# The order of a quad's seven products, and of their weights

## The chip, the cores and the metric

The kernel runs on one core of one Trainium2 chip. Its time is the device time of one execution in microseconds (us), given as the median of several runs; lower is better. A profile is one further execution, recorded by the hardware profiler.

Engines are named as in the profile: PE is the matrix engine and PEld its loading of weights, DVE the vector engine, ACT the scalar engine, POOL the general engine, SP the engine that issues most transfers. Matrix products build up in eight banks of PSUM, each 128 partitions by 512 floats.

## The reference

One layer of a streaming encoder over 2048 tokens of 1024 features, all in float32. An input projection feeds a chunked band attention and an mLSTM, both gated; their sum goes through an output projection, and a feed-forward block of width 4096 follows.

```python
xn = rms_norm(x, mix_norm_g)
proj = xn @ w_in
aq, ak, av, mq, mk, mv, mo, ipre, fpre, ga, gm = jnp.split(proj, points, axis=-1)
att = chunk_band_attention(aq, ak, av, rel_bias)
...
mlstm_out = sigmoid(mo) * rms_norm(mlstm_chunkwise(conv(mq), conv(mk), mv, ipre, fpre))
y = sigmoid(ga) * (att @ w_att_proj) + sigmoid(gm) * (mlstm_out @ w_mlstm_proj)
x = x + y @ w_out
hn = rms_norm(x, ffn_norm_g)
x = x + jnp.square(jax.nn.relu(hn @ w_up)) @ w_down
```

## The kernel before, in words

The tokens are cut into four blocks of 512. Blocks 0 and 1 form one span, blocks 2 and 3 the other. The large products of a span (gates, the second span's input projections, output projection, up and down projection) are computed by Winograd's form of Strassen's scheme: a product of 2 x 2 blocks by seven products in place of eight. Each float32 operand is split in two parts, high and low, and each product takes three matmuls.

**A quad** (`quad`, L731, matmul at L753) is one such set of seven products: 0 to 6. For one product it takes one weight tile (`next_w`), runs over two halves n of the output features, over four tiles k of the inner dimension and over the three pairs of parts: 24 matmuls of 128 x 512. A product goes to banks named by `PLACES` (L64): product 0 to x, 1 to y, 2 to z, 3 to x, 4 to z, 5 and 6 to x. A place has two banks, one for each half. Products that share a place add to what stands there; before such a product begins, what the place held must have been taken out (the event `clear`). Order of the seven products before: 0, 1, 2, 3, 4, 5, 6, so places x y z x z x x.

**Emptying the banks** (`combine`, L1876). After products 0, 2 and 3 ACT copies the bank to a buffer of the pool `ctx` (L1887). After products 1, 4 and 5 DVE adds the bank to one of these copies (L1895): 1 to the copy of 0, 4 to the copy of 3, 5 to the copy of 2. Product 6 is the last output. Banks y are given back after product 1, z after 4, x after 6. For the output projection (`after_out`, L2074) DVE adds the bank to a tile of x in place of the copy (L2109).

**A token quad** (`quad_tok`, L760, matmul at L781) computes values of the attention and the mLSTM. It differs in that a product needs two weight tiles, and goes through both halves first with one tile and then with the other.

**Weights.** A weight tile of a product is 128 x 1024. ACT casts it to its high part (L608) and DVE subtracts to get the low part (L610, `split_now`); the result lies in one of three buffers `wsp`. Its source lies in one of four buffers `wraw`. Where a quad's weights come from raw tiles (`quad_w`, L614), four tiles a, b, c, d are loaded (L567) and the sums that the scheme needs are made in place by four DVE subtractions (L627), between the splits. In six quads of the first up projection (`kept`) each sum is also written to HBM (L622), and the tile is overwritten only after that. Other quads load ready tiles one by one (`part`); their sums were made earlier by `sum_w` (L544, subtractions at L559), which DVE does in between. `weights` (L479) lists all tiles in the order in which PE takes them.

**Order of the work.** Threads (generators) run in a simulated flow with estimated costs (`Flow`). That gives buffers and the order on PE. Then `Order` (L212) lists each other engine's instructions anew, by due times counted back from PE and with margins, and fixes that order; each engine works through its list in order, SP's transfers too.

**Stages with quads:** four gate quads of span 0 (`ga0`, `ga1`, `gm0`, `gm1`), two output quads, eleven of span 1's input (`gm0`, `gm1`, `q`, `mq`, the token quad `vm0`, `ga0`, `k`, the token quad `vm1`, `mk`, `ga1`, `mo`), eight up quads, then after the down projection two output quads and eight up quads of span 1. In all 33 quads and two token quads, 168 matmuls each. In a stage's first quad the operands come in while it runs. The down projection (matmuls at L669 to L671) is worked otherwise.

Of the kernel before, what the change touches and what calls it, by code (L numbers as in the profile page):

```python
# [57 lines left out]
EARLY_SUMS.update({i: N_Q - N_F + n for n, i in enumerate((7, 9, 11, 12, 13, 14, 15, 16))})  # L58

ORDER = (0, 1, 3, 2, 5, 4, 6)  # L60
N_RING = 8
LAST = (3, 1)

# [309 lines left out]
class Layer:  # L373
# [105 lines left out]
    def weights(self):  # L479


        part = lambda q, m: ("part", (q, m))
        quad = lambda name: ("quad", (int(name[2]) if name[:2] == "gm" else Q_IN[name], False))
        proj = [("plain", N_W - 8 + 4 * x + j) for j in (0, 2, 1, 3) for x in range(2)]
        rows = lambda *k: [("plain", 8 + 5 * j + i) for j in range(4) for i in k]
        mv = [("plain", n) for n in range(4, 8)]
        for b in range(2):
            yield from (("plain", n) for n in range(4))
            yield from mv + rows(0, 1) if b == 0 else rows(0, 1) + mv
            yield from rows(2, 3) + rows(4)  # L490
        yield from proj
        for name in GATES:
            yield quad(name)
        yield from proj
        yield from (part(q, m) for q in range(N_G, N_G + N_O) for m in range(7))
        for name in IN_ORDER:
            if name[:2] == "vm":
                yield from (part(Q_VM + kk, m) for m in range(7) for kk in range(2))
            else:
                yield quad(name)  # L500
        for s in range(NS):
            if s == 1:
                yield from (part(q, m) for q in range(N_G, N_G + N_O) for m in range(7))
            for q in range(N_G + N_O, N_G + N_O + N_F):
                if s == 0 and q >= N_G + N_O + N_USUM:
                    yield "quad", (q, True)
                else:
                    yield from (part(q, m) for m in range(7))
            for p, m in enumerate(ORDER):
                for q in range(N_Q - N_F, N_Q):  # L510
                    yield part(q, m)
            if s == 0:
                yield from proj + proj

    def loader(self):
        fl, io = self.fl, self.io
        i = 0
        for kind, n in self.weights():
            if kind == "quad":
                raws, evs = [], [Event() for _ in range(4)]  # L520
                fl.spawn(self.quad_w(i, *n, raws, evs), 0)
                for j in range(4):
                    (raw,) = yield "get", self.wraw, 1
                    raws.append(raw)
                    fl.spawn(self.load_w(io["wf"][n[0], j], raw, evs[j]), 0)
                i += 7
                continue
            first = kind == "plain" and i < KT // 2
            if kind == "plain":
                src = io["w"][n]  # L530
            else:
                q, m = n
# [78 lines left out]
        self.wtile[i] = w  # L611
        fl.set(self.wev[i])

    def quad_w(self, i, q, kept, raws, evs):  # L614


        fl, V = self.fl, self.nc.vector
        spilt = [Event() for _ in range(4)]

        def keep(n, raw):  # L620
            yield "sp", 1750, 2000
            self.nc.sync.dma_start(self.td[q].ap()[n], raw)  # L622
            fl.set(spilt[n])

        def sub(n, dst, x, y):
            yield "dve", dve_ns(1024)
            V.tensor_sub(dst, x, y)  # L627
            if kept:
                fl.spawn(keep(n, dst), 1)
            else:  # L630
                fl.set(spilt[n])

        yield "wait", [evs[0]]
        a = raws[0]
        yield from self.split_now(i, a)
        yield "wait", [evs[1]]
        b = raws[1]
        yield from sub(0, a, b, a)
        yield "wait", [evs[2]]
        c = raws[2]  # L640
        yield from self.split_now(i + 1, c)
        yield from self.split_now(i + 2, a)
        yield "wait", [evs[3], spilt[0]]
        d = raws[3]
        yield from sub(1, a, d, a)
        yield from self.split_now(i + 3, a)
        yield from self.split_now(i + 4, d)
        yield from sub(2, b, d, b)
        fl.put(self.wraw, d, late=self.LATE)
        yield "wait", [spilt[1]]  # L650
        yield from sub(3, a, c, a)
# [76 lines left out]
        fl.put(self.wsplit, w, late=self.LATE_SPLIT)  # L728
        return got

    def quad(self, A, aev, after, release):  # L731


        fl = self.fl
        bank, clear = {}, {}
        mm = self.nc.tensor.matmul
        for m, z in enumerate(PLACES):
            w = yield from self.next_w()
            wv = w.rearrange("p a (k n c) -> p a k n c", k=4, n=2)
            for n in range(2):  # L740
                new = (z, n) not in bank
                if new:
                    (bank[z, n],) = yield "get", self.banks, 1
                else:
                    yield "wait", [clear[z, n]]
                ps = bank[z, n]
                for k in range(4):
                    if aev[m][k] is not None:
                        yield "wait", [aev[m][k]]
                    yield "pe", 681  # L750
                    a = A[m][k]
                    for x, y in ((0, 0), (0, 1), (1, 0)):
                        mm(ps, wv[:, x, k, n], a[:, y], start=new and k == 0 and x == y == 0,  # L753
                           stop=k == 3 and x == 1, skip_group_check=True)
                clear[z, n] = after(m, n, ps)
            fl.put(self.wsplit, w, late=self.LATE_SPLIT)
            if release:
                fl.put(self.rpool, *A[m])

    def quad_tok(self, p, A, aev, after):  # L760
# [1 line left out]
        fl = self.fl  # L762
        bank, clear = {}, {}
        mm = self.nc.tensor.matmul
        for m, z in enumerate(PLACES):
            for kk in range(2):
                w = yield from self.next_w()
                wv = w.rearrange("p a (k c) -> p a k c", k=2)
# [44 lines left out]
    def dense(self):  # L813
# [59 lines left out]
        for i, name in enumerate(GATES):  # L873
            last = name == GATES[-1]
            if 0 < i < 3:
                fl.spawn(self.sum_w(N_G + i - 1), 3)
            if last:
                fl.spawn(self.take_mix(1), 1)
            yield from self.quad(*G, self.after_in(name, 0), release=last)
        O, first_out = yield from self.project_span(0, None)  # L880
        for i in range(N_O):
            if i == N_O - 1:
                ready, read = Event(), [Event() for _ in range(4)]
                fl.spawn(self.rows_far(ready, read), 1)
                for k in range(4):
                    fl.spawn(self.take_x(k, *X, ready, read), 2)
            yield from self.quad(*O, self.after_out(0, i, None) if i > 0 else first_out, release=i == N_O - 1)

        for i, name in enumerate(IN_ORDER):
            if i in EARLY_SUMS:  # L890
# [7 lines left out]
            if name[:2] == "vm":  # L898
                yield from self.quad_tok(int(name[2]), *X, self.after_vm(int(name[2])))
            else:  # L900
                yield from self.quad(*X, self.after_in(name, 1), release=last)
        for s in range(NS):
            if s == 1:
                for i in range(N_O):
                    if i == N_O - 1:
                        for k in range(2):
                            fl.spawn(self.take_x2(1, k, *U), 2)
                    yield from self.quad(*O, self.after_out(1, i, U) if i > 0 else first_out, release=i == N_O - 1)
            for i in range(N_F):
                if s == 0 and len(IN_ORDER) + i in EARLY_SUMS:  # L910
                    fl.spawn(self.sum_w(EARLY_SUMS[len(IN_ORDER) + i]), 3)
# [15 lines left out]
                yield from self.quad(*U, self.after_up(s, i), release=i == N_F - 1)  # L927
            if s == 0:
                for h in range(2):
                    for j in range(KT):  # L930
# [1684 lines left out]
```

## Time and profile before

| what | value |
|---|---|
| median of 3 runs | 2777.7 us |
| lowest and highest run | 2773.86 and 2778.86 us |
| the profiled execution's own time | 2772.18 us |
| its span | 2770.4 us |
| PE busy | 2750.6 us, 13006 matmuls |
| DVE busy | 2054.3 us |
| ACT busy | 1492.5 us |
| moved by transfers | 678.64 MB, mean 245 GB/s |

The span goes from the first to the last instruction. A row of the profile names line, engine, operation, what is written and read, the count, then the time and, in brackets, how long the engine was idle before it and what ended that. The end of a matmul is modelled: matmuls overlap by it, so that a row of one matmul is longer than the step from one to the next. Waits are listed as the waiting engine and line, the releaser, the sum in us, how often, and the longest.

### The profile page before, as it was taken

The numbers are of one execution on the slowest core, as the hardware profiler recorded it, in microseconds if no ns is written. First come the engines' busy times: TensorE is split into PE (matmuls) and PEld (weight loads), VectorE is DVE, ScalarE is ACT, GpSimd is POOL, SyncE is SP. The second block draws the span as 40 slices with busy tenths as digits, with TensorE's granted clock in tenths as the row PEclk, the third lists the DMA queues.
The fourth block names the chain that finished last, engine by engine and source line by source line (L and its number), as shares of the span: only waits on it lengthen the run. The fifth ranks groups of instructions, "written<-read, shape, count | busy, mean of one in ns | idle before, by whom it ended". The sixth has DMA issues, their size and how long they took to land.

```text
span 2770.4 us, 38619 instructions
## 1 busy us (share of the span) xinstructions
PE 2750.6 (99%) x13006; PEld 2284.9 (82%) x13006; DVE 2054.3 (74%) x3785; ACT 1492.5 (54%) x2609; POOL 53.8 (2%) x100
## 2 busy tenths in 40 slices
PE   9999999999999999999999999999999999999998
PEld 7788888888778878888888888888888888888887
DVE  7796788768996866886676688889888656555565
ACT  5564576535454535575555566666335655554443
POOL 0010001000000000000000000000000000000000
PEclk9999999999999999999999999999999999999999
DMA  8968759768765677588878977877877667766574
GB/s 284 291 197 270 233 160 304 248 224 320 258 205 203 221 250 256 194 275 325 289 278 278 298 235 232 258 228 234 291 247 256 207 220 262 243 237 219 190 229 151
DMA packets 329190, 678.64 MB, mean 245 GB/s; under 512 B 36856, under 2 KB 67744, under 8 KB 328992
## 3 DMA queue, kind: packets, MB, share of 16 engines
q1 hardware_dynamic: 328848, 676.17, 73.4%
q8 instruction: 102, 1.67, 0.3%
q14 instruction: 96, 0.79, 0.1%
q10 hardware_dynamic: 144, 0.01, 0.0%
HBM read 472.59 MB, written 203.44 MB: 244 GB/s over the span
## 4 chain that ended last, share of the span: by engine, by line
PE 89%; DMA 5%; DVE 3%; issue 2%; ACT 1%; SPq 0%; POOL 0%; POOLq 0%; DVEq 0%; ACTq 0%
PE bank L753 45%; PE bank L669 11%; PE bank L670 11%; PE bank L671 11%; PE bank L1443 2%; PE bank L1416 2%; PE bank L781 2%; PE bank L1474 2%; DMA r<-mfar 1%; DMA r<-u 1%; DVE wsp L610 1%; PE bank L1728 0%; PE bank L1729 0%; PE bank L1730 0%; PE bank L1714 0%
## 5 line engine op out<-in xcount | busy, mean ns | idle before, releaser
L753 PE MATMUL bank<-r,wsp 128*128 128x512 f32 x5544 | 1265.0, 390 | 0.7 <-DVE ctx L2109 0.3
L753 PEld LDWEIGHTS bank<-r,wsp 128*128 128x128 f32 x5544 | 1038.2, 188 | 221.2 <-DVE ctx L1895 2.6
L610 DVE TENSOR_TENSOR wsp<-wraw,wsp 128x1024 fp32r<-128x1024 f32 x458 | 559.6, 1222 | 353.6 <-ACT wsp L608 336.5
L608 ACT CAST wsp<-wraw 128x1024 fp32r<-128x1024 f32 x458 | 481.3, 1051 | 507.2 <-PE bank L670 220.3
L669 PE MATMUL bank<-r,wsp 128*128 128x512 f32 x1472 | 586.1, 398 | 0.8 <-ACT r L1252 0.6
L670 PE MATMUL bank<-r,wsp 128*128 128x512 f32 x1472 | 574.9, 391 | 0.2 <-DVE r L1257 0.2
L671 PE MATMUL bank<-r,wsp 128*128 128x512 f32 x1472 | 574.8, 391 | 0.0
L671 PEld LDWEIGHTS bank<-r,wsp 128*128 128x128 f32 x1472 | 276.3, 188 | 58.4
L669 PEld LDWEIGHTS bank<-r,wsp 128*128 128x128 f32 x1472 | 276.7, 188 | 52.9 <-ACT r L1252 0.9
L670 PEld LDWEIGHTS bank<-r,wsp 128*128 128x128 f32 x1472 | 277.0, 188 | 50.8 <-DVE r L1257 0.5
L1895 DVE TENSOR_TENSOR ctx<-bank,ctx 128x512 f32<-128x512 f32 x186 | 126.9, 687 | 90.4 <-PE bank L753 90.2
L1257 DVE TENSOR_TENSOR r<-r 128x512 fp32r<-128x512 f32 x248 | 164.7, 686 | 20.3 <-ACT r L1252 19.9
L1252 ACT CAST r<-r 128x512 fp32r<-128x512 f32 x248 | 148.9, 620 | 44.8 <-DMA r<-u 41.5
L1887 ACT COPY ctx<-bank 128x512 f32<-128x512 f32 x186 | 107.9, 581 | 65.0 <-PE bank L753 61.2
L1458 ACT ACTIVATE sc<-sc,scs 128x640 f32<-128x640 f32 (+4 forms) x128 | 97.4, 763 | 62.2 <-DVE scs L1455 56.3
L2226 ACT ACTIVATE ctx<-ctx 128x512 f32<-128x512 f32 x96 | 60.6, 631 | 102.3 <-DVE ctx L1895 102.3
L1479 DVE TENSOR_TENSOR r<-bank,r 128x512 fp32r<-128x512 f32 (+1 forms) x168 | 97.0, 595 | 19.1 <-ACT r L1477 18.4
L1449 DVE CUSTOM_DVE_ANT_0 sc<-bank,bias 128x320 f32<-128x320 f32 (+3 forms) x240 | 103.4, 461 | 6.9 <-PE bank L1443 4.9
L1477 ACT CAST r<-bank 128x512 fp32r<-128x512 f32 (+1 forms) x168 | 82.1, 518 | 35.8 <-PE bank L1474 31.1
L1416 PE MATMUL bank<-r,r 128*128 128x512 f32 x336 | 94.8, 363 | 3.2 <-DVE r L1479 3.2
L627 DVE TENSOR_TENSOR wraw<-wraw,wraw 128x1024 f32<-128x1024 f32 x76 | 92.8, 1223 | 2.0
L559 DVE TENSOR_TENSOR ctx<-ctx,ctx 128x512 f32<-128x512 f32 x112 | 76.3, 686 | 19.1 <-DMA ctx<-in_wf 14.1
(263 smaller groups left out, 2721.1 us busy)
## 6 DMA issues: line engine op xcount, KB each, us to landing
wraw<-in_wf SPq DMA_DIRECT2D x178, 512.0 KB, 4.3
wraw<-wsum SPq DMA_DIRECT2D x136, 512.0 KB, 4.3
r<-u SPq DMA_DIRECT2D x224, 256.0 KB, 4.2
wraw<-in_w SPq DMA_DIRECT2D x87, 512.0 KB, 5.7
u<-ctx SPq DMA_DIRECT2D x128, 256.0 KB, 2.2
ctx<-in_wf SPq DMA_DIRECT2D x112, 256.0 KB, 5.0
wsum<-ctx SPq DMA_DIRECT2D x112, 256.0 KB, 3.5
u<-tmp SPq DMA_DIRECT2D x96, 256.0 KB, 3.6
```

The costliest lines, as they stand in the source:

```text
L608: nc.scalar.copy(w[:, 0], raw)
L610: nc.vector.tensor_sub(w[:, 1], raw, w[:, 0].bitcast(F32))
L669: mm(ps, lh, rh, start=first, stop=False)
L670: mm(ps, lh, rl, start=False, stop=False)
L671: mm(ps, ll, rh, start=False, stop=last)
L753: mm(ps, wv[:, x, k, n], a[:, y], start=new and k == 0 and x == y == 0, stop=k == 3 and x == 1, skip_group_check=True)
L1252: self.nc.scalar.copy(dst[:, 0], src)
L1257: self.nc.vector.tensor_sub(dst[:, 1], src, dst[:, 0].bitcast(F32))
L1416: nc.tensor.matmul(acc[:, :, c0:c0 + w], st, sl[:, :, o:o + w], start=n == 0, stop=n == total - 1)
L1449: nc.vector.tensor_tensor_reduce(out=e[:, x * w:x * w + w], in0=bks[x][:, :w], in1=br[:, j0 + x * w:j0 + x * w + w], op0=ALU.add, op1=ALU. ...
L1887: nc.scalar.copy(t[:, o:o + 512], ps)
L1895: nc.vector.tensor_add(t[:, o:o + 512], ps, t[:, o:o + 512])
```

## The change

Quads and token quads go through their products in the order 0, 2, 3, 1, 5, 4, 6 (`APART`), places x z x y x z x. The first quad of each stage keeps the order 0 to 6 (`PLAIN`): the first gate quad, the first output quad of each span, the first input quad, the first up quad of each span, six in all. Weights are listed and made in the order of the products. Where a quad makes its sums itself, the four raw tiles are loaded in the order a, b, d, c, and the chain of subtractions and splits is written anew: the second subtraction, for product 3, now comes after the split of the first sum (product 2), with the split of c (product 1) behind it. Nothing is added or left out of the computation.

```diff
+PLAIN, APART = (0, 1, 2, 3, 4, 5, 6), (0, 2, 3, 1, 5, 4, 6)
...
         for name in GATES:
-            yield quad(name)
+            yield quad(name, PLAIN if name == GATES[0] else APART)
...
             if name[:2] == "vm":
-                yield from (part(Q_VM + kk, m) for m in range(7) for kk in range(2))
+                yield from (part(Q_VM + kk, m) for m in APART for kk in range(2))
...
                 if s == 0 and q >= N_G + N_O + N_USUM:
-                    yield "quad", (q, True)
+                    yield "quad", (q, True, APART)
                 else:
-                    yield from (part(q, m) for m in range(7))
+                    yield from (part(q, m) for m in (PLAIN if q == N_G + N_O else APART))
...
-                for j in range(4):
+                for j in (0, 1, 2, 3) if n[2] is PLAIN else (0, 1, 3, 2):
                     (raw,) = yield "get", self.wraw, 1
-                    raws.append(raw)
+                    raws[j] = raw
...
     def quad_w(self, i, q, kept, seq, raws, evs):
...
         yield from sub(0, a, b, a)
+        if seq is APART:
+            yield from self.split_now(i + 1, a)
+            yield "wait", [evs[3], spilt[0]]
+            d = raws[3]
+            yield from sub(1, a, d, a)
+            yield from self.split_now(i + 2, a)
+            yield "wait", [evs[2]]
+            c = raws[2]
+            yield from self.split_now(i + 3, c)
+            yield from sub(2, b, d, b)
+            yield from self.split_now(i + 4, b)
+            yield from self.split_now(i + 5, d)
+            fl.put(self.wraw, d, late=self.LATE)
+            yield "wait", [spilt[1]]
+            yield from sub(3, a, c, a)
+            fl.put(self.wraw, c, late=self.LATE)
+            yield "wait", [spilt[2]]
+            fl.put(self.wraw, b, late=self.LATE)
+            yield from self.split_now(i + 6, a)
+            yield "wait", [spilt[3]]
+            fl.put(self.wraw, a, late=self.LATE)
+            return
...
-    def quad(self, A, aev, after, release):
+    def quad(self, A, aev, after, release, seq=APART):
...
-        for m, z in enumerate(PLACES):
+        for m in seq:
+            z = PLACES[m]
...
     def quad_tok(self, p, A, aev, after):
...
-        for m, z in enumerate(PLACES):
+        for m in APART:
+            z = PLACES[m]
...
-            yield from self.quad(*G, self.after_in(name, 0), release=last)
+            yield from self.quad(*G, self.after_in(name, 0), release=last, seq=PLAIN if i == 0 else APART)
```

The other calls of `quad` in `dense` are changed like the last one.

More of the change, by code (lines that the diff above doesn't have):

```diff
@@ L482, in weights @@
         part = lambda q, m: ("part", (q, m))
-        quad = lambda name: ("quad", (int(name[2]) if name[:2] == "gm" else Q_IN[name], False))
+        quad = lambda name, seq=APART: ("quad", (int(name[2]) if name[:2] == "gm" else Q_IN[name], False, seq))
         proj = [("plain", N_W - 8 + 4 * x + j) for j in (0, 2, 1, 3) for x in range(2)]
@@ L492, in weights @@
         for name in GATES:
-            yield quad(name)
+            yield quad(name, PLAIN if name == GATES[0] else APART)
         yield from proj
-        yield from (part(q, m) for q in range(N_G, N_G + N_O) for m in range(7))
+        yield from (part(q, m) for q, seq in ((N_G, PLAIN), (N_G + 1, APART)) for m in seq)
         for name in IN_ORDER:
             if name[:2] == "vm":
-                yield from (part(Q_VM + kk, m) for m in range(7) for kk in range(2))
+                yield from (part(Q_VM + kk, m) for m in APART for kk in range(2))
             else:
-                yield quad(name)
+                yield quad(name, PLAIN if name == IN_ORDER[0] else APART)
         for s in range(NS):
             if s == 1:
-                yield from (part(q, m) for q in range(N_G, N_G + N_O) for m in range(7))
+                yield from (part(q, m) for q, seq in ((N_G, PLAIN), (N_G + 1, APART)) for m in seq)
             for q in range(N_G + N_O, N_G + N_O + N_F):
                 if s == 0 and q >= N_G + N_O + N_USUM:
-                    yield "quad", (q, True)
+                    yield "quad", (q, True, APART)
                 else:
-                    yield from (part(q, m) for m in range(7))
+                    yield from (part(q, m) for m in (PLAIN if q == N_G + N_O else APART))
             for p, m in enumerate(ORDER):
@@ L519, in loader @@
             if kind == "quad":
-                raws, evs = [], [Event() for _ in range(4)]
+                raws, evs = {}, [Event() for _ in range(4)]
                 fl.spawn(self.quad_w(i, *n, raws, evs), 0)
-                for j in range(4):
+                for j in (0, 1, 2, 3) if n[2] is PLAIN else (0, 1, 3, 2):
                     (raw,) = yield "get", self.wraw, 1
-                    raws.append(raw)
+                    raws[j] = raw
                     fl.spawn(self.load_w(io["wf"][n[0], j], raw, evs[j]), 0)
@@ L612, in split_now, with quad_w @@
         fl.set(self.wev[i])
-    def quad_w(self, i, q, kept, raws, evs):
+    def quad_w(self, i, q, kept, seq, raws, evs):
         fl, V = self.fl, self.nc.vector
@@ L886, in dense @@
                     fl.spawn(self.take_x(k, *X, ready, read), 2)
-            yield from self.quad(*O, self.after_out(0, i, None) if i > 0 else first_out, release=i == N_O - 1)
+            yield from self.quad(*O, self.after_out(0, i, None) if i > 0 else first_out, release=i == N_O - 1,
+                                 seq=PLAIN if i == 0 else APART)
         for i, name in enumerate(IN_ORDER):
@@ L900, in dense @@
             else:
-                yield from self.quad(*X, self.after_in(name, 1), release=last)
+                yield from self.quad(*X, self.after_in(name, 1), release=last, seq=PLAIN if i == 0 else APART)
         for s in range(NS):
@@ L907, in dense @@
                             fl.spawn(self.take_x2(1, k, *U), 2)
-                    yield from self.quad(*O, self.after_out(1, i, U) if i > 0 else first_out, release=i == N_O - 1)
+                    yield from self.quad(*O, self.after_out(1, i, U) if i > 0 else first_out, release=i == N_O - 1,
+                                         seq=PLAIN if i == 0 else APART)
             for i in range(N_F):
@@ L926, in dense @@
                         fl.spawn(self.attention_far(b), 1)
-                yield from self.quad(*U, self.after_up(s, i), release=i == N_F - 1)
+                yield from self.quad(*U, self.after_up(s, i), release=i == N_F - 1, seq=PLAIN if i == 0 else APART)
             if s == 0:
```

## The prediction, made before the changed kernel was run

> **What bounds the kernel now.** I read the page's first two parts, then what the matrix engine (PE) waits for, then one line's waiters, then the timeline around the stalls that these named.
>
> ```profile
> span 2770.4 us, 38619 instructions
> PE 2750.6 (99%) x13006; PEld 2284.9 (82%) x13006; DVE 2054.3 (74%) x3785; ACT 1492.5 (54%) x2609; POOL 53.8 (2%) x100
> PEclk9999999999999999999999999999999999999999
> ```
>
> PE is busy 2750.6 of 2770.4 us, at the full granted clock in all slices. The change leaves the number of matmuls as it is, so all that it can win is time in which PE stands: the 19.8 us that are left, and short stalls that the modelled ends of matmuls hide, which have to be found from starts.
>
> The second view, who waited for whom, for PE alone, over the whole span:
>
> ```profile
> PE bank L1416 <- DVE r L1479: 3.2, 2, 2.4
> PE bank L781 <- DVE ctx L1895: 2.1, 2, 1.7
> ...
> PE bank L753 <- DVE ctx L2109: 0.3, 1, 0.3
> ...
> PE bank L753 <- ACT r L1254: 0.2, 1, 0.2
> PE bank L753 <- DVE r L1259: 0.2, 1, 0.2
> ```
>
> L753 is the quads' matmul and L781 the token quads'. Their named waits sum to 2.8 us. The 0.7 us at L753 belong to three operands and one sum of the first output quad, which keeps its order. What is left is 2.1 us, in two places, both for L1895, the VectorE (DVE) addition that empties a bank. The same line seen from its waiters:
>
> ```profile
> L1895 DVE TENSOR_TENSOR ctx<-bank,ctx x186: 676/684/693, 512.4 to 2445.3; 128x512 f32<-128x512 f32 x186
> ...
> who waited for it (us, times):
> ...
>   PEld bank L753: 2.6, 9
>   PE bank L781: 2.1, 2
> ```
>
> So weight loading (PEld) of ordinary quads also waited nine times for it, 2.6 us in all.
>
> **What the change touches.** Product 5 and product 6 of a quad both build in the x banks. The timeline gives the pace and the stalls:
>
> ```profile
> 503.50 38.46 PE L753 MATMUL bank<-r,wsp 128*128 128x512 f32 x168
> 541.82 114.73 PE L753 MATMUL bank<-r,wsp 128*128 128x512 f32 x504
> 967.65 4.24 PE L781 MATMUL bank<-wsp,r 128*128 128x512 f32 x18
> 973.59 5.71 PE L781 MATMUL bank<-wsp,r 128*128 128x512 f32 x24 [1.70 <-DVE ctx L1895]
> 1084.73 3.56 PE L781 MATMUL bank<-wsp,r 128*128 128x512 f32 x15
> 1088.67 5.72 PE L781 MATMUL bank<-wsp,r 128*128 128x512 f32 x24 [0.38 <-DVE ctx L1895]
> 1094.23 113.95 PE L753 MATMUL bank<-r,wsp 128*128 128x512 f32 x502
> ```
>
> The last row runs without a stall: less the last matmul's modelled 0.39 us it is 113.56 us for 501 steps, 0.2267 us each. A quad has 168 matmuls, 38.08 us; a product 24, 5.44 us.
>
> In the old order the first x bank is complete when product 5's second half begins, and product 6 wants it back when that half ends: 12 x 0.2267 = 2.72 us, in which DVE must start and run 0.684 us. A token quad goes through both banks twice per product, which leaves six matmuls, 1.36 us. In the new order 0, 2, 3, 1, 5, 4, 6 (banks x z x y x z x) a whole product of another bank always lies between: 2.72 + 5.44 = 8.16 us, and 1.36 + 5.44 = 6.80 us in a token quad. These are the margins of the change.
>
> *Token quads, both in the new order.* Without a stall the 24 matmuls would have begun at 967.65 + 18 x 0.2267 = 971.73, so the first stall is 973.59 - 971.73 = 1.86 us; the second is 1088.67 - (1084.73 + 15 x 0.2267) = 0.54 us. Sum 2.40 us; the listed 2.1 us is short by the modelled ends. Why the first was so long stands in DVE's timeline:
>
> ```profile
> 967.58 1.23 DVE L610 TENSOR_TENSOR wsp<-wraw,wsp 128x1024 fp32r<-128x1024 f32 x1 [0.25 <-ACT wsp L608]
> 970.29 1.42 DVE L559 TENSOR_TENSOR ctx<-ctx,ctx 128x512 f32<-128x512 f32 x2 [1.49 <-DMA wsum<-ctx]
> 971.63 1.22 DVE L610 TENSOR_TENSOR wsp<-wraw,wsp 128x1024 fp32r<-128x1024 f32 x1
> 972.76 0.68 DVE L1895 TENSOR_TENSOR ctx<-bank,ctx 128x512 f32<-128x512 f32 x1
> ```
>
> DVE stood on a store of weight sums, then did three queued operations, then emptied the bank. With 6.80 us of margin all of that fits. What is late next is the weights: counting L610 in the order of the products, those of product 6 were ready at 967.58 + 1.23 = 968.81 and 971.63 + 1.22 = 972.85, and without the stall they are wanted at 971.73 and 971.73 + 2.72 = 974.45. Spare 2.9 and 1.6 us, so nothing takes the stall's place here and I book all 2.40 us.
>
> *Ordinary quads.* 27 of 33 change (the first of each of six stages does not). Nine waits of PEld, mean 2.6 / 9 = 0.29 us, bound their loss from above; no idle time of PE for L1895 at L753 bounds it from below at nothing. The rows between: the first row above is a quad with 38.46 - 0.39 - 167 x 0.2267 = 0.2 us too much, the second three quads with 114.73 - 0.39 - 503 x 0.2267 = 0.3 us. I take 0.15 us each, nearer those rows, and eight of the nine, since a first quad keeps its own: 8 x 0.15 = 1.2 us.
>
> *Weights in the new order.* The same seven splits and four subtractions per quad, and the same four loads, with the last two exchanged. But in the six quads of the first up projection that write their sums to HBM, the second subtraction overwrites the first's result, and now stands one product earlier behind that store. One such quad, from the timeline, and the store's landing:
>
> ```profile
> 1314.31 2.49 DVE L627 TENSOR_TENSOR wraw<-wraw,wraw 128x1024 f32<-128x1024 f32 x2
> 1315.56 1.58 SPq L622 DMA_DIRECT2D wsum<-wraw  x2
> 1317.45 22.54 PEld L753 LDWEIGHTS bank<-r,wsp 128*128 128x128 f32 x100 [0.28 <-DVE ctx L1895]
> 1319.70 1.23 DVE L610 TENSOR_TENSOR wsp<-wraw,wsp 128x1024 fp32r<-128x1024 f32 x1 [1.38 <-ACT wsp L608]
> 1322.99 1.06 ACT L608 CAST wsp<-wraw 128x1024 fp32r<-128x1024 f32 x1 [0.98 <-PE bank L753]
> 1324.58 1.22 DVE L610 TENSOR_TENSOR wsp<-wraw,wsp 128x1024 fp32r<-128x1024 f32 x1
> DMA to landing us min/median/max: 2.6/3.2/4.2
> ```
>
> The store lands by 1315.56 + 4.2 = 1319.8; the second product's split ends at 1320.93; the second subtraction can then run to 1322.2, before the third product's cast at 1322.99. The split after it ends at 1325.8. These weights are for the quad that begins six quads after the last row of the pace, at 1094.23 + 6 x 38.08 = 1322.7, so its third product begins at 1322.7 + 2 x 5.44 = 1333.6. So 0.8 us of cover, and behind it 7.8 us of lead; past both, each us late would cost six. I book nothing. Queued behind a waiting subtraction on DVE would be bank additions, which now have 8.16 us. SP issues the same loads and stores; a quad's first raw buffer comes free one split (5.44 us) later than before, and the same lead of 7.8 us covers that.
>
> *Buffers.* Product 0's copy waits three products for its partner in place of one, and the copies of products 2 and 3 begin a product earlier, so two to four of the sixteen ctx buffers are held longer, and y and z banks come free later in a quad. A copy has 8.16 us before its bank is wanted; I book nothing, with up to 1 us in either direction from the re-laid plan.
>
> **The sum.** 2.40 + 1.2 = 3.6 us less (bounds 2.1 and 2.4 + 2.6 = 5.0). The profiled execution took 2772.18 us, its span and 1.8 us around it; it becomes 2768.6. The three runs had a median of 2777.7 (2773.86 to 2778.86), so the profiled one is 5.5 us quicker than usual. On the median's scale: 2777.7 - 3.6 = 2774.1 us, 0.13%. A measurement of this kernel tells about 0.2% (5.5 us) from no change, so this counts as within it.
>
> A rule to weigh: the Trainium skill, in "Perfetto Trace Analysis", section "Optimizing Tensor Performance", says that independent groups of matmuls should go round different banks, so that the emptying of one lies beside the next group's matmuls. By it alone each of the 29 reordered quads would win an exposed emptying. The trace does not agree: the quad's second half already covers it but for the 2.1 us and the nine short waits.
>
> **The rivals.**
>
> *More than the profiled run shows.* The 5.5 us by which the usual run is longer may lie at these handoffs, whose 2.72 us are the thinnest margin in a quad. If all of it goes too, the gain is 9.1 us, if half, 6.4: 2768.6 to 2771.4, say 2770.0. For it speaks that nine waits are near the edge; against it that nothing shows where those 5.5 us are.
>
> *All emptyings exposed.* 29 x 0.684 = 19.8 us, 2757.9 us; the named waits speak against it. This is the rule of the Trainium skill above.
>
> *Nothing nets.* The stalls come back as others of the same size in the re-laid plan, since every instruction after 503 us gets a new place: 2777.7 us. Against it: all margins named above.
>
> *Slower: the stall of the token quads moves to their weights.* There a weight lasts only 2.72 us and spares of 1.6 to 2.9 us stand ahead. DVE still serves the weight sums in order, and their store can take long, from the chain of waits:
>
> ```profile
> 963.51 6.76 DMA wsum<-ctx
> ```
>
> A DVE that stands through such a landing in both token quads costs up to 2 x (6.76 - 1.6) = 10.3 us in weights; less 3.6, that is 6.7 us slower, 2784.4. It decides from 1.6 us of standing on, and is slower than before from 3.6 us in sum. For it: DVE did stand 1.49 us there. Against it: that cost the weights nothing.
>
> *The clock.* The lowest granted clock in windows of 100 us is that of the last (window, its length, busy us of PE, PEld, DVE, ACT and POOL, granted clock, DMA):
>
> ```profile
> 2700.00:2770.00 70.00, 61.65 (x302) 51.59 (x300) 40.29 (x57) 27.55 (x41) 2.02 (x2) 0.96 0.45 155
> ```
>
> Were it 0.96 through the 35 quads, 1333 us x 4% = 53 us would be added: 2831. The old order already goes round three banks at full clock. The Trainium skill, in "TensorE: Matmul & The Clock Gate", section "A second HAM failure mode: psum-queue depth-cycling", tells of a kernel whose clock swung because PE idled shortly between groups as it cycled through banks; no slice here shows that.
>
> **How the numbers follow.** Forecast 0.50; more than the profile shows 0.22; all exposed 0.02; nothing nets 0.14; weights of the token quads 0.11, of which 0.07 beyond 0.2%; clock 0.01. Faster by over 0.2%: 0.22 + 0.02 = 0.24. Slower: 0.07 + 0.01 = 0.08. Within: 0.50 + 0.14 + 0.04 = 0.68. The range goes from 2768.0, the whole of the larger gain, to 2781.0, which holds the case of no gain with the scatter of the runs and the milder half of the slower one; 0.15 is left out.
>
> **What would show it.** In the new trace: no wait at L781 for L1895; PEld's waits at L753 for L1895 down from nine to one or two; the token quads at 38.1 us each in place of 40.0 and 38.7 (start to start); the first output quad's 0.7 us of waits still there; PE's busy time the same within 1 us. The prediction is wrong if L753 or L781 waits for a split of weights (L610) or for a copy (L1887), or if the gain lies in a stage without quads.

## The result, and the profile after

| kernel | median | lowest and highest | ratio to before |
|---|---|---|---|
| before, 22 runs | 2776.18 us | 2771.73 to 2780.34 | |
| changed, 22 runs | 2772.13 us | 2768.99 to 2775.56 | 0.9987, interval 0.9981 to 0.9992 |

The change wins 4.05 us, 0.13%. The forecast was 3.6 us, within 0.2% of no change.

The profiled execution of the changed kernel took 2772.80 us. The page's first lines:

```profile
span 2771.0 us, 38596 instructions
...
PE 2748.9 (99%) x13006; PEld 2285.9 (82%) x13006; DVE 2059.0 (74%) x3785; ACT 1489.5 (54%) x2609; POOL 51.5 (2%) x100
...
PEclk9999999999999999999999999999999999999999
```

Its span is 0.6 us longer than that of the profile before, although the median fell by 4.05 us. One profiled execution on each side does not show a difference of this size; its stalls have to be read place by place. In the changed file the quads' matmul is L777 (L753 before), the token quads' L806 (L781), the bank addition L1922 (L1895), the copy of a bank L1914 (L1887), the cast of an operand L1279 (L1252). What PE waited for, over the whole span:

```profile
PE bank L692 <- ACT r L1279: 2.9, 1, 2.9
...
PE bank L777 <- ACT r L1279: 1.3, 1, 1.3
...
PE bank L777 <- ACT ctx L1914: 0.9, 1, 0.9
...
PE bank L777 <- DVE r L1284: 0.2, 1, 0.2
```

There is no row for L806: the token quads' 2.1 us are gone. So are the three waits of the first output quad. New are a wait for a copy (0.9 us), for operands (1.3 and 0.2 us), and a longer one at the start of the down projection (2.9 us). The waiters of the bank addition:

```profile
L1922 DVE TENSOR_TENSOR ctx<-bank,ctx x186: 674/691/693, 512.4 to 2445.9; 128x512 f32<-128x512 f32 x186
...
who waited for it (us, times):
...
  PEld bank L777: 0.5, 2
```

Nine waits of PEld, 2.6 us, have become two, 0.5 us. Both lie in quads that keep the old order, the first gate quad and the first up quad of span 1. Then PE's timeline, where the token quads and the two new stalls stand:

```profile
936.52 38.40 PE L806 MATMUL bank<-wsp,r 128*128 128x512 f32 x168
974.76 5.60 PE L777 MATMUL bank<-r,wsp 128*128 128x512 f32 x24
...
1050.92 38.24 PE L806 MATMUL bank<-wsp,r 128*128 128x512 f32 x168
1089.00 3.33 PE L777 MATMUL bank<-r,wsp 128*128 128x512 f32 x14
...
1152.66 59.00 PE L777 MATMUL bank<-r,wsp 128*128 128x512 f32 x259 [0.94 <-ACT ctx L1914]
1212.94 0.50 PE L777 MATMUL bank<-r,wsp 128*128 128x512 f32 x1 [1.28 <-ACT r L1279]
1213.66 46.58 PE L777 MATMUL bank<-r,wsp 128*128 128x512 f32 x204 [0.22 <-DVE r L1284]
```

From start to start the token quads take 974.76 - 936.52 = 38.24 and 1089.00 - 1050.92 = 38.08 us, in place of 40.0 and 38.7. The quad behind the second one begins at 1089.00, 5.2 us ahead of the 1094.23 of before. Of that, 3.3 us are given back within 125 us: the first stall lies in the quad ga1, the two others in the first up quad. To put numbers on stalls that modelled ends hide, I took the steps between the starts of successive matmuls, less 0.2267 us, and summed them per quad:

| lost in, us | before | changed |
|---|---|---|
| two token quads | 1.97 + 0.66 | 0.16 + 0.00 |
| seven reordered quads with a short wait | 1.71 in sum | 0.28 in sum |
| of that at the handoff from product 5 to 6 | 1.1 in sum | 0.00 |
| first output quad (old order in both) | 2.05 | 0.00 |
| input quad ga1 | 0.00 | 1.23 |
| first up quad (old order in both) | 0.00 | 2.11 |

The rest of the 1.71 and the 0.28 us lies beside small matmuls of other work that fall into these quads.

From the first matmul of the gate quads to that of the last up quad before the down projection it is 976.05 us before and 973.94 us after. So the quads of these two executions differ by 2.1 us; the median's 4.05 us have an interval of 2.2 to 5.3 us. This stretch, called the quads' stretch below, holds 4295 matmuls in every trace here, so it can be compared from kernel to kernel; in a second execution of the changed kernel it was 973.62 us. What the median wins beyond it is not located: outside this stretch the changed kernel's profile is 2.7 us longer than that of before, and the profiled execution of before was 4.0 us quicker than its median.

### The profile page after: what moved, and what is told of

The parts are those of the page before. It is cut to its first block, busy times and chain, and to the rows that moved or that the text cites. A ratio compares the mean times of both kernels' runs of the same rounds, so it can differ in the third digit from the quotient of the medians.

```text
span 2771.0 us, 38596 instructions
## 1 busy us (share of the span) xinstructions
PE 2748.9 (99%) x13006; PEld 2285.9 (82%) x13006; DVE 2059.0 (74%) x3785; ACT 1489.5 (54%) x2609; POOL 51.5 (2%) x100
## 4 chain that ended last, share of the span: by engine, by line
PE 92%; DVE 3%; DMA 2%; issue 2%; ACT 1%; SPq 0%; POOLq 0%; POOL 0%; DVEq 0%; ACTq 0%
PE bank L777 42%; PE bank L692 12%; PE bank L694 12%; PE bank L693 12%; PE bank L806 3%; PE bank L1470 2%; PE bank L1443 2%; PE bank L1501 2%; DVE wsp L611 1%; DVE ctx L2093 1%; DMA r<-mfar 1%; PE bank L1741 0%; PE bank L1756 0%; PE bank L1757 0%; PE bank L1755 0%
## 5 line engine op out<-in xcount | busy, mean ns | idle before, releaser
L777 PE MATMUL bank<-r,wsp 128*128 128x512 f32 x5544 | 1264.2, 390 | 2.4 <-ACT r L1279 1.3
L777 PEld LDWEIGHTS bank<-r,wsp 128*128 128x128 f32 x5544 | 1038.8, 188 | 220.3 <-ACT r L1279 1.7
L1922 DVE TENSOR_TENSOR ctx<-bank,ctx 128x512 f32<-128x512 f32 x186 | 127.3, 688 | 100.3 <-PE bank L777 99.9
L1279 ACT CAST r<-r 128x512 fp32r<-128x512 f32 x248 | 148.6, 622 | 51.9 <-DMA r<-u 48.8
L1914 ACT COPY ctx<-bank 128x512 f32<-128x512 f32 x186 | 107.9, 581 | 83.2 <-PE bank L777 70.5
```

The costliest lines, as they stand in the source:

```text
L1279: self.nc.scalar.copy(dst[:, 0], src)
L1914: nc.scalar.copy(t[:, o:o + 512], ps)
L1922: nc.vector.tensor_add(t[:, o:o + 512], ps, t[:, o:o + 512])
```

## The experiments

Theory one is that of the forecast: the time goes at the handoff of the x banks. Theory two is its rival that nothing nets, because the plan is laid anew. Theory three, formed from the changed kernel's profile, says that the new order gives some results out later and so makes the two new stalls. Each kernel was timed in five rounds beside the kernel before on the same chip; times are medians.

**The token quads alone.**

```diff
-PLAIN, APART = (0, 1, 2, 3, 4, 5, 6), (0, 2, 3, 1, 5, 4, 6)
+PLAIN, TOKEN = (0, 1, 2, 3, 4, 5, 6), (0, 2, 3, 1, 5, 4, 6)
+APART = PLAIN
```

> Only the two token quads take the new order; the 33 ordinary quads keep 0 to 6. If the handoff of the x banks costs the time (theory one), the two waits of the token quads for the bank additions (1.86 and 0.54 us in the profile of before) go and nothing else does: 2.4 us faster, ratio 0.9991, and the nine short waits of weight loading at the ordinary quads stay. If the time comes from the re-laid plan (theory two), the ratio can be anything from 0.998 to 1.002 and the stages that lose or gain are others. If only the ordinary quads count, 1.0000.

Measured: 2774.25 us against 2774.05, ratio 0.9998 (0.9990 to 1.0007). In the trace both token stalls are gone, 0.00 us each. But four ordinary quads, all in the old order, lose 1.2 us that they did not lose before: mk 0.63, the gate quad gm1 0.28, mq 0.20 and mo 0.13 us, each at the start of product 6. So the quads' stretch is 974.79 us, 1.3 us shorter in place of 2.4: the plan, laid anew, has exposed other handoffs of the same kind. The interval holds theory one's 0.9991 and no change as well, so the time decides nothing here; the trace shows the mechanism.

**The ordinary quads alone.** The token quads' order is set back to `PLAIN`, the rest as in the change.

> Only the ordinary quads, without the first of each stage, take the new order; the token quads keep 0 to 6. Theory one: the short waits go, 1.2 us faster (bounds 0 to 2.6), ratio 0.9996, and one to two waits of the token quads for the bank additions stay, 0.5 to 1.9 us each. Together with the run of the token quads alone it should give the whole change, 0.9987. Theory two: no such sum, each of the two lies anywhere from 0.998 to 1.002.

Measured: 2773.99 us, ratio 1.0000 (0.9991 to 1.0008). PE's waits in the stages with quads, 490 to 1520 us:

```profile
PE bank L806 <- DVE ctx L1922: 2.0, 2, 1.6
PE bank L777 <- ACT r L1279: 1.3, 1, 1.3
PE bank L777 <- ACT ctx L1914: 0.9, 1, 0.9
...
PE bank L777 <- DVE r L1284: 0.2, 1, 0.2
```

The token quads' waits stay, as theory one said, and both new stalls of the changed kernel are here, 1.23 and 2.03 us by starts. So they come with the ordinary quads. The first output quad loses nothing here either: the ordinary quads' order took that loss away too. In sum these parts nearly cancel (976.21 us in the quads' stretch), which is what the ratio says; the two runs do not add up to 0.9987, but their intervals are too wide to tell. In the stretch they make -1.3 and +0.2 us against the whole change's -2.1; the four handoffs that opened in the run of the token quads alone cost nothing in the changed kernel, where those quads have the new order too.

**A new plan alone.** The kernel before with one number of the planner:

```diff
-    LATE, LATE_SPLIT = 3000.0, 2500.0
+    LATE, LATE_SPLIT = 3000.0, 2400.0
```

> The kernel before with one number of the planner changed, the assumed lateness of a freed weight buffer, 2400 in place of 2500. No quad changes its order; the order of the other work on every engine is laid anew. It measures what a new plan alone does. Theory one: below 1 us either way, ratio 0.9996 to 1.0004, with the waits for the bank additions still there in about the same number. Theory two: a move of 2 to 4 us, ratio 0.9985 to 1.0015.

Measured: 2785.65 us, ratio 1.0040 (1.0028 to 1.0053). Both theories had expected less. The token quads' waits stay (2.41 and 0.66 us by starts). Most of the loss lies ahead of all quads: the span is 13.5 us longer than in the profile before, and the first gate quad begins at 512.8 us, 9.3 us later. The quads' stretch is 1.4 us longer (977.46 us). Three windows ahead of the quads (window, length, busy us of PE, PEld, DVE, ACT and POOL, granted clock, DMA), then three of the kernel before, of which the first lies 10 us earlier, where its own gap is:

```profile
115.00:125.00 10.00, 8.33 (x39) 6.72 (x38) 6.41 (x20) 7.47 (x18) 0.29 (x2) 0.83 0.89 282
215.00:225.00 10.00, 7.96 (x41) 6.66 (x40) 5.93 (x12) 5.99 (x17) 1.22 (x1) 0.83 1.09 369
475.00:485.00 10.00, 8.18 (x34) 6.38 (x33) 7.57 (x16) 6.44 (x16) 1.81 (x2) 0.83 0.51 179
```

```profile
105.00:115.00 10.00, 7.63 (x46) 6.47 (x45) 6.45 (x24) 4.08 (x12) 0.00 (x0) 1.00 1.08 271
215.00:225.00 10.00, 9.85 (x49) 7.81 (x48) 4.88 (x12) 3.87 (x11) 1.82 (x1) 1.00 1.07 359
475.00:485.00 10.00, 10.00 (x49) 8.33 (x49) 9.03 (x22) 7.29 (x21) 1.38 (x1) 1.00 0.99 360
```

In the first three windows, where PE stood for 1.7 to 2.0 us, the granted clock was 0.83 over the window. A plan can thus move this kernel by 11 us, three times what the change moves it by: theory two is possible in size, though not shown.

**More neighbours in the token quads.** `TOKEN` is `(0, 1, 2, 3, 5, 6, 4)`, the rest as before.

> The token quads alone go in the order 0, 1, 2, 3, 5, 6, 4, banks x y z x x x z, so that two handoffs per token quad are between neighbours in place of one; ordinary quads as before. Theory one: the stalls of the token quads about double, from 2.4 to 3.5 to 5 us, 1 to 2.5 us slower, ratio 1.0004 to 1.0009, with waits at the third-last and second-last product. Theory two: no tie between these waits and the time.

Measured: 2777.47 us, ratio 1.0013 (1.0004 to 1.0022). Slower, as expected, but not for the reason given. The waits, 490 to 1520 us:

```profile
PE bank L807 <- DVE ctx L1923: 0.8, 2, 0.4
PE bank L778 <- DVE ctx L1923: 0.6, 1, 0.6
PE bank L807 <- ACT ctx L1915: 0.4, 1, 0.4
```

A wait for the copy has come between the new neighbours, and the waits for the addition are still there, but the long one has shrunk: the two quads lose 2.14 us by starts and not 3.5 to 5. The added handoff costs 0.60 us by starts in one token quad and nothing in the other; the old one costs 0.58 and 0.54 us, where the first had cost 1.86. The loss of time lies elsewhere: the quads' stretch is 1.3 us longer (977.37 us), and quads whose order was not touched lose more, the gate quad gm1 0.94 us in place of nothing, again at its product 6 (L778 above).

**The weight sums kept out of the token quads,** all orders as before:

```diff
-EARLY_SUMS = {1: Q_VM, 2: Q_VM + 1, 4: N_G + N_O, 5: N_G + N_O + 1}
-EARLY_SUMS.update({i: N_Q - N_F + n for n, i in enumerate((7, 9, 11, 12, 13, 14, 15, 16))})
+EARLY_SUMS = {1: Q_VM, 2: Q_VM + 1, 5: N_G + N_O, 8: N_G + N_O + 1}
+EARLY_SUMS.update({i: N_Q - N_F + n for n, i in enumerate((9, 10, 11, 12, 13, 14, 15, 16))})
```

> The kernel before, all orders old, but the weight sums whose subtractions (L559) DVE did within the first token quad start after it, and none starts in the second. Theory one says that 1.86 us of stall came because DVE stood on a store of these sums with the bank addition queued behind: the first token quad's wait falls from 1.86 to 0.5 us or less, like the second's, without any change of order; ratio 0.9990 to 0.9998. If the wait stays at 1.5 us or more, the sums were not its cause. The re-laid plan can move other stages by some us.

Measured: 2781.36 us, ratio 1.0022 (1.0013 to 1.0030).

```profile
PE bank L753 <- ACT r L1252: 3.0, 1, 3.0
...
PE bank L753 <- DVE ctx L1895: 1.2, 2, 0.9
PE bank L781 <- DVE ctx L1895: 0.8, 2, 0.4
```

The first token quad's wait fell from 1.7 to 0.4 us, as theory one said, or from 1.86 to 0.54 us by starts, which is what the second token quad's handoff costs too: the subtraction that stood on a transfer was what made it long. The time came out the other way than expected, and as a remedy it fails. The first up quad now waits 3.0 us for its operands, and the quads' stretch is 7.5 us longer (983.54 us). That the moved sums take ctx buffers and DVE from others there is argued; two more of the sums were moved with them.

**The changed kernel under the other plan** (2400 in place of 2500):

> The changed kernel with the planner's number 2400 in place of 2500, as in the run e3 of the kernel before, which was 0.4% slower. If the order gains its time under any plan (theory one), this stands 0.10 to 0.15% under e3: ratio 1.0025 to 1.003, with no wait at the token quads. If what counts is the plan of the first 503 us, which the order does not touch, it is slower than before by about what e3 was, and the difference between the two is anything. If the change removed what e3 lost, 0.999.

Measured: 2780.54 us, ratio 1.0018 (1.0009 to 1.0027), against 1.0040 (1.0028 to 1.0053) for the kernel before under that plan. The two were run on different chips, each beside the kernel before. So the order's gain shows under a second plan too, about 0.2%, and the traces bear it out where the order acts: the quads' stretch is 971.70 us against 977.46. ga1's stall is there (1.23 us), the first up quad's is not: that one depends on the plan as well.

**First quads in the new order too.** `seq=APART` for every quad, and weights to match.

> The changed kernel with the first quad of each stage in the new order too (six more). Theory one: the one short wait left in the first gate quad goes (0.2 us). Against it stand the operands of a stage's first quad, which come in the order 0, 1, 2: products 2 and 3 are then wanted one product earlier, so the first output quad and the first up quads should wait for operands, 1 to 5 us each in two to four of the six: ratio 0.999 to 1.004, slower than the change. If the operands are early enough, 0.9987.

Measured: 2774.52 us, ratio 0.9996 (0.9987 to 1.0005).

```profile
PE bank L777 <- ACT r L1279: 3.8, 1, 3.8
PE bank L777 <- ACT ctx L1914: 0.9, 1, 0.9
```

Of the six first quads only one pays: the first up quad loses 5.79 us by starts in place of 2.11. Of these, 3.95 us are the stand, and most of the rest comes from a slower clock behind it (see the last section). The first gate quad's short wait at its handoff is gone, as expected; 0.09 us is left beside a small matmul of other work. For the other first quads the old order was not needed in this execution.

**Which quads make the new stalls.** Four kernels are the changed one with some input quads back in the old order, the first of them with ga1 and mo:

```diff
-                yield quad(name, PLAIN if name == IN_ORDER[0] else APART)
+                yield quad(name, PLAIN if name in (IN_ORDER[0], "ga1", "mo") else APART)
```

(with `seq` in `dense` to match), the others with mk alone, mo alone, and all three. With the last three ran the change itself once more.

> The changed kernel, but the last two input quads of span 1 (ga1 and mo) keep the old order. Theory three: there the new order holds ctx buffers longer, so that a copy (L1914 in the changed kernel) comes 1.24 us late in ga1 and the operands of the first up quad 2.1 us late; with the old order both stalls go and at most two short handoff waits of 0.2 us come back: 3 us faster than the changed kernel, ratio to the kernel before 0.9975 to 0.998. If the two stalls come from the re-laid plan or from transfers, they stay, ratio 0.9987 as for the change.

> The changed kernel once more, beside the next three on one chip. If its new stalls in ga1 (1.24 us, the copy L1914) and in the first up quad (2.1 us, operands) belong to the plan, they are there again within 0.3 us; if they were chance of one execution, they are not. The stall of 2.9 us at the start of the down projection (L692), of which the kernels so far showed 0.6 to 3.5 us, should be another than 2.9. Ratio 0.9987.

> The changed kernel with the quad mk alone in the old order. In the new order mk's first outputs come two products later, so that its eight convolutions on DVE fall into ga1. Theory three a (late outputs of mk delay ga1): ga1's stall goes, the first up quad's 2.1 us stay; 1 to 1.5 us faster than the changed kernel on the same chip, ratio 0.9982. If ga1 itself holds too many ctx buffers, ga1's 1.24 us stay and the ratio is 0.9987.

> The changed kernel with the quad mo alone in the old order. Theory three b (mo's buffers come free later, so that the operands of the first up quad are loaded later): the first up quad's 2.1 us go, ga1's 1.24 us stay; 2 us faster than the changed kernel, ratio 0.9980. If ga1 was what delayed the operands, they stay, 0.9987.

> The changed kernel with mk, ga1 and mo in the old order. Theories three a and b together: both stalls go, and the handoff wait of 1.5 us that ga1 had in the run with ga1 and mo in the old order goes too, since it stood behind mk's convolutions; 3 us faster than the changed kernel, ratio 0.9975, the fastest of all. If the two theories are wrong, 0.9987 with a stall in ga1 or the first up quad.

| old order in | lost in ga1, us | in the first up quad, us | quads' stretch, us | median, us | ratio and interval |
|---|---|---|---|---|---|
| ga1, mo | 1.51 | 0.00 | 972.43 | 2769.15 | 0.9978 (0.9969 to 0.9987) |
| none, once more | 1.23 | 1.85 | 973.62 | 2771.45 | 0.9986 (0.9977 to 0.9995) |
| mk | 0.00 | 1.45 | 972.01 | 2771.07 | 0.9985 (0.9976 to 0.9994) |
| mo | 1.27 | 0.00 | 972.35 | 2768.20 | 0.9975 (0.9965 to 0.9985) |
| mk, ga1, mo | 1.09 | 0.00 | 971.69 | 2769.91 | 0.9974 (0.9965 to 0.9983) |

The last four were run on one chip. PE's waits there, 490 to 1520 us, for mk in the old order, then for mo:

```profile
PE bank L777 <- ACT r L1280: 0.7, 1, 0.7
```

```profile
PE bank L777 <- ACT ctx L1915: 0.9, 1, 0.9
```

Each of the two takes away one stall and leaves the other, as theories three a and b said. So mk in the new order makes ga1's stall, and mo in the new order that of the first up quad. In the times only mo shows: its median is 3.3 us under that of the changed kernel beside it, mk's 0.4 us, though 1 to 1.5 were expected; in the quads' stretch both are shorter, by 1.3 and 1.6 us. The changed kernel's stalls come again in a second execution (1.23 and 1.85 us), so they are the plan's and not chance. The stall at the start of the down projection was 2.4 us this time, 2.9 the first: that one varies with the execution.

With ga1 in the old order, the expectation for it fails twice:

```profile
PE bank L777 <- DVE ctx L1923: 1.2, 1, 1.2
```

```profile
PE bank L777 <- DVE ctx L1923: 0.8, 1, 0.8
```

These are the runs with ga1 and mo, and with all three. ga1 then has its neighbours again and waits at the old handoff, 1.2 and 0.8 us, though in the kernel before it did not. That mk's convolutions stood in front was my reason in the expectation, but with mk in the old order too the wait is still 0.8 us. DVE's timeline of that run shows what does stand in front:

```profile
1159.96 1.23 DVE L628 TENSOR_TENSOR wraw<-wraw,wraw 128x1024 f32<-128x1024 f32 x1 [0.94 <-DMA wraw<-in_wf]
1161.11 1.28 DVE L1923 TENSOR_TENSOR ctx<-bank,ctx 128x512 f32<-128x512 f32 x2
```

DVE stood 0.94 us on the load of a weight tile, subtracted, and only then emptied the bank; PE went on at 1161.84. This is much like the first token quad before the change. The traces suggest mk and mo in the old order and ga1 in the new one; that was not run.

How mk makes ga1 late is seen in the timeline of the changed kernel, in ga1:

```profile
1147.67 1.53 DVE L2093 SCALAR_TENSOR_TENSOR ctx<-ctx,cvw,ctx 128x512 f32<-128x512 f32 x2
...
1149.12 0.68 DVE L1922 TENSOR_TENSOR ctx<-bank,ctx 128x512 f32<-128x512 f32 x1
...
1149.84 0.63 ACT L2055 ACTIVATE ctx<-ctx 128x512 f32<-128x512 f32 x1 [1.82 <-DVE ctx L1922]
...
1152.03 0.58 ACT L1914 COPY ctx<-bank 128x512 f32<-128x512 f32 x1
...
1152.66 0.73 PE L777 MATMUL bank<-r,wsp 128*128 128x512 f32 x2 [0.94 <-ACT ctx L1914]
```

L2093 is the convolution of mk's results. In the new order mk's first result is out after its fourth product in place of its second, so the convolutions of mk lie within ga1. DVE does them ahead of a bank addition; ACT stands 1.82 us on that addition, and the copy that PE needs is queued behind on ACT, with two more operations between. Its bank was complete at about 1143.5 and PE wanted it at 1151.6; the copy began at 1152.03, so 8.16 us of cover were not enough.

mo's results are stored from ctx buffers, and the operands of the first up quad are loaded into ctx buffers. The last such load in the changed kernel, and what PE's operand waited for:

```profile
1206.60 0.51 SPq L1872 DMA_DIRECT2D ctx<-x  x1
```

```profile
1211.52 0.72 ACT L1879 ACTIVATE ctx<-ctx,gcol 128x512 f32<-128x512 f32 x1 [0.98 <-DMA ctx<-x]
1212.27 1.34 ACT L1279 CAST r<-ctx 128x512 fp32r<-128x512 f32 x2
```

The load is issued at 1206.60, 2.1 us after the quad has begun (1204.5), its tile is scaled at 1211.52, and the cast behind it releases PE at 1212.94. With mo in the old order the last of these loads stands far earlier:

```profile
1183.55 0.42 SPq L1873 DMA_DIRECT2D ctx<-x  x1
```

That is 20.9 us ahead of the quad (1204.4), and the stall is gone; with mk alone in the old order the load is 2.1 us behind the start again, and the stall is there. So the late load makes the stall. Why it is late is open: a buffer that comes free late is argued from the code and from mo's part in it, no run changed the number of buffers, and under the other plan the load is 21.1 us ahead with mo in the new order.

## Why the prediction was right, and where its steps were not

- The size was near: 3.6 us forecast, 4.05 measured (2.2 to 5.3), within 0.2% as said. In part that is luck: the traces show 2.1 and 2.4 us of it in the quads, and the rest is not located. The time of 2772.13 us lies in the range and 2.0 us under the forecast of 2774.1; 1.5 us of that is the median of before, 2776.18 in 22 runs against 2777.7 in the three shown.
- The step for the token quads was right. 2.40 us were booked, 2.47 us went by starts. The weights of product 6, for which it worked out the splits, were ready. What is left, 0.16 us, goes with a wait of PEld for another weight, at the fourth product of the first token quad, which the prediction did not look at.
- The step for the ordinary quads was right in size: 1.2 us booked, 1.1 us gone at the handoffs of seven quads, 0.16 each, where 0.15 was taken for each of eight. Of the nine waits of PEld one lay in the first gate quad, and one, in mk, cost nothing by starts.
- The steps on weights were right but for that one wait. PE waited for no split in the quads, the longer way round the stores in the up quads included:

```profile
PEld bank L806 <- DVE wsp L611: 0.2, 1, 0.2
```

- The step that failed is "Buffers", booked at nothing with up to 1 us either way. It saw that copies and tiles are held longer, but priced it only by the 8.16 us of a copy's bank, without what is queued ahead on ACT and DVE. In ga1 the copy began 8.5 us after its bank was complete, and PE stood. What was missed is who else waits: a quad's results come later (the first after the fourth product in place of the second), and behind mk and mo there is work that follows from them. That it was mk and mo is shown by the runs; that mo acts through its buffers is not. It cost 1.23 + 2.11 = 3.3 us. A wait for a copy was named as a sign of being wrong, and it came.
- A second miss has the other sign. The first output quad was to keep its waits; it lost 2.05 us before and 0.00 after. It is gone in all eight kernels whose ordinary quads have the new order, under both plans, and there in all five that have the old one, so it comes with that order. Through which of its operands is not settled.
- The two misses, 3.3 us lost and 2.05 won, largely cancel: 2.5 + 1.1 + 2.05 - 3.3 = 2.3 us, and the quads' stretch was 2.1 us shorter. That is why the sum looks better than its steps.
- Of the rivals: that the gain was larger than the profiled run showed is not excluded, since the interval reaches 5.3 us, nor shown. That all emptyings were exposed is out. That the weights of the token quads take over the stall is out: these quads run at pace but for the 0.16 us. That nothing nets was nearer than 0.14 says: half of the token quads' gain went at other handoffs when they were changed alone, and a plan's own moves go up to 11 us, though the order's gain was there under two plans.
- PE's busy time was to stay within 1 us and fell by 1.7. That sign was chosen badly, since modelled ends count short stalls as busy time.

## What to carry to other kernels

A better order inside a stage changes when its results come out, not only what it waits for. List who takes the first and the last result, and which buffers they hold, and keep the old order where something is queued behind it: here mo alone in the old order made 0.9975 out of 0.9986 on one chip, with intervals that overlap. A margin in time counts only less what is queued ahead of the operation that has to meet it. Where another part of the program is planned by the same list, run a plan that is changed for no reason beside the change, to know what a new plan alone does.

## What the runs showed of the hardware

The granted clock fell to half after some short stands of PE. In the changed kernel at the start of the down projection, and at the same place before:

```profile
1540.00:1550.00 10.00, 7.12 (x28) 5.39 (x27) 5.38 (x15) 3.17 (x6) 0.00 (x0) 0.83 1.03 393
```

```profile
1540.00:1550.00 10.00, 9.15 (x41) 7.06 (x41) 6.37 (x9) 3.13 (x5) 2.06 (x1) 1.00 1.05 397
```

The trace has 3.41 us at a clock of 0.50 there, right behind the 2.9 us that PE stood, which makes 0.83 over the 10 us. About 3.41 / 2 = 1.7 us are lost by it on top, an estimate. What it does to matmuls shows in the run with all quads in the new order, behind the stand of the first up quad:

```profile
1215.70:1219.00 3.30, 3.30 (x9) 2.42 (x8) 3.23 (x6) 1.96 (x4) 0.00 (x0) 0.50 0.78 271
```

Here matmuls start 0.43 us apart in place of 0.2267. So a stall can cost more than its length. It does not follow from the length alone: before, PE stood 10 - 7.63 = 2.4 us between 105 and 115 us at a clock of 1.00, and in the run with mk alone in the old order two stands of 2.6 us had no drop behind them either; under the other plan 1.8 us between 475 and 485 us were followed by 0.83. The Trainium skill, in "TensorE: Matmul & The Clock Gate", section "HAM oscillation — how this bites in real kernels", gives as a rule that PE should not idle for more than about 3.4 us; here the clock fell to half behind stands of about 1.7 to 2.9 us.
